# A hybrid recurrent layer on one core: a PSUM bank for the merges of the inverses, the last norm in three groups, another order of rows in the output product

## The chip, the cores and the metric

The kernel runs on one core of one Trainium2 chip. The metric is the device time of one execution in microseconds, smaller is better; comparisons use the median of several runs.

## The reference

One layer over a prompt of 1024 tokens and 8 sample tokens that go on from carried states, D = 1024:

```
h = RMSNorm(x);  p = h @ W_in
mixed = concat[GLA(p), S5(p), GatedDeltaNet(p), RWKV7(p)]     # 256 columns each, each times SiLU of its own gate path
x = x + mixed @ W_out
y = RMSNorm(x) * final_g
```

All four mixers are causal recurrences over the tokens. GatedDeltaNet (GDN) and RWKV7 are computed in chunks of 64 tokens; each chunk needs the inverse of a unit triangular 64 x 64 matrix. The outputs are y for all 1032 tokens and the last states of every mixer.

## The kernel before

**Tiling.** The tokens are taken in two halves: 512, and 512 plus the 8 samples (520). In the code the second half's steps are marked by an apostrophe. Every product with a weight matrix is a *stream* (`stream`, L269): a weight slice of 1024 x 128 is loaded in two chunks of four blocks (256 KB each), split by ScalarE (`wh`, L265) and GpSimd (`wl`, L266) into a high and a low part, and multiplied in three passes, 24 matmuls for each piece of columns (L277). With 520 columns there are two pieces of 260 and 48 matmuls. `proj` streams the normed input; `out_stream` (L1272) streams the gated branch outputs against W_out, transposes the result back and hands it on.

**Stages.** Each mixer is made of units (R RWKV, D GDN, L GLA, S S5), two pairs of heads each, that run in stages: 0 projections, 1 preparation, 2 the inverse, 3 the scan over chunks (GLA: stage 2 is the scan). A gate `g` is visited twice: first its projection, then the norm of the branch output and its product with the gate (`gated`, L1210). W is the preparation of the S5 weights, `x` the norm of the input, `T` the output product (`tail_first` for the first half, `tail` for the second), `y` the scaling of the first half's rows (`rows_first`). `x'` loads its rows with an order constraint behind the last matmul issued before it, and its result `xhi` takes the one buffer that the first half's projections read.

**Order.** The string ORDER (L33) is the order in which the stages are written down, and with that their priority; PRI (L32) raises single stages by a number of places. A planner built into the framework then lays out the queue of each engine from priorities, from dependencies and from the buffers of each tag that are free (NB, L25). So the order on an engine isn't the order of the string, and each engine works off its own queue strictly in order.

**Inverses.** `inverse` (L287) inverts the 32 x 32 diagonal blocks on VectorE (31 steps, L307 and L309), sends them through DRAM into XT, transposes them into Dn (L318), and merges them: for each of two 64-row groups p a product `pq` (L323), a copy (L324), a product `po` (L326) and a copy into XT (L327). There are 8 inverses (two pairs of RWKV and GDN in two halves). `pq` and `po` are tiles of the psc pool, which has four PSUM banks; the scans of RWKV, GDN and GLA (L471 to L501, L679 to L704, L820 to L829) and the transposes of the output streams (L1282) use the same pool. Of the eight banks two are for psp (streams), two for psb.

**The end.** In `tail` (L1320) the result of each of 8 output streams is added to x in columns of 128 (L1345). After the seventh stream (896 columns) `squares` sums squares on ScalarE and multiplies by final_g on VectorE; after the eighth it does so for the last 128 columns. Then the norm's factor is made on five small columns, each row group is scaled and stored.

The matmuls in a stream take the 128-row blocks k of the branch outputs in the order 0 to 7: GLA (0, 1), S5 (2, 3), GDN (4, 5), RWKV (6, 7). Before the matmuls `out_parts` splits each block into ohi (L1268) and olo; its loop order GORD is RWKV, GDN, GLA, S5.

Of the kernel before, what the change touches and what calls it, by code (L numbers as in the profile page):

```python
# [8 lines left out]
F32 = mybir.dt.float32  # L9
F32R = mybir.dt.float32r  # L10
I32 = mybir.dt.int32
AF = mybir.ActivationFunctionType
ALU = mybir.AluOpType
# [9 lines left out]
HALF = T // 2  # L23
NH = HALF + NS
NB = dict(ta=9, pr=11, on=3, gp=8, sh=2, kA=6, XT=2, Gt=5, s8=4, ss=4, wr=3, wh=2, wl=2, d1=1, LT=1, DT=2, DP=1, d2=2, Dn=2, w8=2, rf=1,  # L25
          fx=3, bv=2, Bn=2, UV=2, r=3, dr=2, gcn=2, ben=2, kdn=2, U=3, at=2, s5i=1, s5h=3, nst=2, psp=2, psb=2, psc=4)
CT_WA, CT_R, CT_SM, CT_G, CT_L, CT_U, CT_GATE = 0, 1, 7, 8, 14, 20, 22
GLA, S5, GDN, RWKV = 0, 1, 2, 3
ENG = dict(kqo="G", kqi="G", qd="G", kds="V", kd="G", rga="G", rgm="V", rcos="G", k2="V", ari="V", aro="V", bko="G", bki="V",
           glu="V", g5="V", cvm="V", l2="V", sgl1="V", sgl2="V", lw0="V", lw1="G", ld0="G", ld1="G", lqk="V", rS="A", rr="V",  # L30
           rU="V", dU="V", fg="V", la="V", tlo="V", cv0="V")
PRI = {"R2": 4000, "D2": 1000, "R3": 4000, "D3": 4000, "L1": 2000, "R1": 600, "L0": 100, "L2": 600, "D0": 300, "D1": 1000}  # L32
ORDER = ("x W W t W m R0 g6 R0 D0 W W M W D0 D1 R1 W R0 R1 R0 L0 R1 L0 R1 D1 L0 g0 D0 D0 S g0 L1 g4 g6 D1 g3 g7 L1 D1 g2 g5 L1 "  # L33
         "x' g7 g1 g4 S t' R1' R1' m' R0' g1 g2 R1' g3 M' R1' R0' D0' g5 R0' D1' D0' L1' g1' g7' R0' D0' D1' g4' g6' D0' L0' L1' "
         "L1' D1' g2' g7' g0' L0' S' D1' g6' g4' L0' g5' g3' S' g3' g0' g1' g5' g2' T y T'")
GORD = ((RWKV, 0), (RWKV, 1), (GDN, 0), (GDN, 1), (GLA, 0), (GLA, 1), (S5, 0), (S5, 1))
GATES = ((GLA, 0), (GLA, 1), (S5, 0), (S5, 1), (GDN, 0), (GDN, 1), (RWKV, 0), (RWKV, 1))
LEVELS = (16, 8, 4, 2, 1)
# [25 lines left out]
def trunk(ctx: ExitStack, tc: tile.TileContext, I, O):  # L64
# [195 lines left out]
    def wsplit(src):  # L260
        raw = wst.tile([128, 4, 128], F32, tag="wr", bufs=NB["wr"], name="wr")
        SP.dma_start(out=raw, in_=src)
        hi = wst.tile([128, 4, 128], F32R, tag="wh", bufs=NB["wh"], name="wh")
        lo = wst.tile([128, 4, 128], F32R, tag="wl", bufs=NB["wl"], name="wl")
        A.copy(hi, raw)  # L265
        G.tensor_tensor(lo, raw, hi, ALU.subtract)  # L266
        return hi, lo

    def stream(wsrc, evac):  # L269

        wt = [wsplit(wsrc[:, 4 * q:4 * q + 4, :]) for q in range(2)]
        for c0, m in X["pieces"] or pieces(X["n"]):
            p = ps_p.tile([128, 512], F32, tag="p", name="psp")
            for k in range(8):
                hi, lo = wt[k // 4]
                for s, (w, x) in enumerate(((hi, X["hi"]), (hi, X["lo"]), (lo, X["hi"]))):
                    X["mm"] = PE.matmul(p[:, :m], w[:, k % 4, :], x[:, k, c0:c0 + m], start=(k == 0 and s == 0), stop=(k == 7 and s == 2))  # L277
            evac(p[:, :m], c0, m)

    def proj(ct, evac):  # L280
# [6 lines left out]
    def inverse(Ga, XT, after):  # L287


        Q = [(p, f) for p in range(2) for f in range(2)]  # L290
        at = lambda p, f: slice(64 * p + 32 * f, 64 * p + 32 * f + 32)
        d1 = drp.tile([2, 2, 8, 32, 32], F32, tag="d1", bufs=NB["d1"], name="d1")
        for p, f in Q:
            r = slice(32 * f, 32 * f + 32)
            nb = 8 // len(Ga[p])
            for b, g in enumerate(Ga[p]):
                SP.dma_start(out=d1[p, f, nb * b:nb * b + nb].rearrange("(c e) s t -> s c e t", e=2), in_=g[r, :, :, r])
        LT = tmp.tile([128, 32, 32], F32, tag="LT", bufs=NB["LT"], name="LT")
# [12 lines left out]
        for q in range(4):  # L311
            SP.dma_start(out=d2.rearrange("p f x (m q) i -> q (p f x) m i", q=4)[q], in_=DT[32 * q:32 * q + 32])
        for p, f in Q:
            SP.dma_start(out=XT[at(p, f), :, 32 * f:32 * f + 32], in_=d2[p, f].rearrange("x c i -> c x i"))
        Dn = tmp.tile([128, 8, 32], F32, tag="Dn", bufs=NB["Dn"], name="Dn")
        for p in range(2):
            late(G.memset(XT[at(p, 1), :, 0:32], 0.0), after)
            V.transpose(Dn[at(p, 0)], XT[at(p, 0), :, 0:32])  # L318
        pq = psc(128, 8, 32)
        po = psc(128, 8, 32)  # L320
        for p in range(2):
            for k in range(8):
                PE.matmul(pq[at(p, 1), k, :], Ga[p][k // nb][0:32, k % nb // 2, k % 2, 32:64], Dn[at(p, 0), k, :], start=True, stop=True)  # L323
            A.copy(Dn[at(p, 1)], pq[at(p, 1)])  # L324
            for k in range(8):
                PE.matmul(po[at(p, 0), k, :], Dn[at(p, 1), k, :], XT[at(p, 1), k, 32:64], start=True, stop=True)  # L326
            A.copy(XT[at(p, 0), :, 32:64], po[at(p, 0)])  # L327
# [944 lines left out]
    def out_stream(m):  # L1272

        yT = tmp.tile([128, NH], F32, tag="sh", bufs=NB["sh"], name="yT")

        def evac(p, c0, k):
            A.copy(yT[:, c0:c0 + k], p)

        stream(I["wo"][m], evac)
        pt = psc(128, 4, 128)  # L1280
        for j in range(4):
            PE.transpose(pt[:, j, :], yT[:, 128 * j:128 * j + 128], ident)  # L1282
        return yT, pt
# [36 lines left out]
    def tail(fgb):  # L1320
        n = NH
        out_parts(1)
        xf = [big(128, D, name="xf") for _ in range(4)]
        for j in range(4):
            late(SP.dma_start(out=xf[j], in_=I["x"][HALF + 128 * j:HALF + 128 * j + 128, :]), X["mm"])
        xs = tmp.tile([128, D], F32, tag="kA", bufs=NB["kA"], name="xs")
        late(SP.dma_start(out=xs[:NS], in_=I["x"][T:TT, :]), X["mm"])
        G1 = 896
        st = tmp.tile([128, 2, 2, 16, 1], F32, tag="nst", bufs=NB["nst"], name="nst")
        rows = [(xf[j], j, 128) for j in range(4)] + [(xs[:NS], 4, NS)]  # L1330

        def squares(g):

            cols = slice(0, G1) if g == 0 else slice(G1, D)
            for x, j, k in rows:
                junk = tmp.tile([128, D], mybir.dt.bfloat16, tag="ta", bufs=NB["ta"], name="junk")
                act(junk[:k, cols], x[:, cols], AF.Square, accum_out=st[:k, 0, g, j])
                tt("fg", x[:, cols], x[:, cols], fgb[:k, cols])

        V.memset(st[:, 0, :, 4], 1.0)  # L1340
        for m in range(8):
            yT, pt = out_stream(m)
            cols = slice(128 * m, 128 * m + 128)
            for j in range(4):
                V.tensor_tensor(xf[j][:, cols], pt[:, j, :], xf[j][:, cols], ALU.add)  # L1345
            pt = psb(128, 128)
            PE.transpose(pt[0:NS], yT[:, HALF:NH], ident)
            V.tensor_tensor(xs[:NS, cols], pt[0:NS], xs[:NS, cols], ALU.add)
            if m == G1 // 128 - 1:
                squares(0)  # L1350
        squares(1)
        w = len(rows)
        ms, t, y = st[:, 0, 0, :w, 0], st[:, 0, 1, :w, 0], st[:, 1, 0, :w, 0]
        V.tensor_tensor(ms, ms, t, ALU.add)
        V.tensor_scalar(ms, ms, 1.0 / D, EPS, ALU.mult, ALU.add)
        rsqrt_small(y, ms, t)
        for x, j, k in rows:
            if j % 2:
                V.tensor_scalar(x, x, y[:k, j:j + 1], None, ALU.mult)
            else:  # L1360
                act(x, x, AF.Copy, scale=y[:k, j:j + 1])
            SP.dma_start(out=O["y"][HALF + 128 * j:HALF + 128 * j + k, :], in_=x)
# [193 lines left out]
```

## Time and profile before

| what | value |
|---|---|
| median of 3 runs | 1075.07 us (1072.87 to 1081.68) |
| the profiled execution | 1080.05 us, its span 1078.3 us |
| TensorE, busy share of the span | 87% |
| TensorE, mean granted clock | 0.847 |
| VectorE / ScalarE / GpSimd, busy share | 65% / 43% / 37% |
| share of the chain that ended last: stream matmuls on TensorE | 20% |
| moved to and from HBM | 95.91 MB, 89 GB/s on average |

The span is the time from the first to the last instruction of the profiled execution. The granted clock is the share of TensorE's full speed (2.4 GHz; the lower level is 1.2) that it was given, averaged over a stretch. A busy TensorE at half clock does half the work.

### The profile page before, as it was taken

To read this page: it belongs to the slowest core of one execution; us is meant where nothing else is said; L and a number is where in the kernel's file an instruction comes from. 1 tells how busy PE (TensorE), PEld (TensorE's weight loads), DVE (VectorE), ACT (ScalarE), POOL (GpSimd) and SP (SyncE) were. 2 spreads that over 40 slices of the span, in tenths; PEclk is the share of its full clock that TensorE was granted. 3 is DMA by queue.
4 is the path that set the end of the run, shared out by engine and by line. 5 is a ranking of instruction groups with operands and counts; after the bars stand their busy time and mean duration, and the time that the engine had idled before them with its cause. 6 is when DMAs were issued, how large, how long until landed. Compare 5 with 4: busy or idle time off the path is not lost.

```text
span 1078.3 us, 17024 instructions
## 1 busy us (share of the span) xinstructions
PE 939.4 (87%) x5994; PEld 770.5 (71%) x5994; DVE 699.1 (65%) x1841; ACT 464.2 (43%) x1079; POOL 394.9 (37%) x434
## 2 busy tenths in 40 slices
PE   3898889979999698897999899988989989797694
PEld 3676657658767486797788777677868967685694
DVE  8628884767636954737578999878975354615614
ACT  4354543322534434532663454554225244257234
POOL 2788653531211441125264313124426311422141
PEclk9999988876868866798999898788889678998697
DMA  7133414220202132134123223211122034536422
GB/s 233 50 129 104 122 53 106 69 59 15 74 25 55 49 99 79 42 116 148 57 80 101 85 76 84 83 41 54 50 69 71 22 118 130 154 112 211 164 79 89
DMA packets 85109, 95.91 MB, mean 89 GB/s; under 512 B 41640, under 2 KB 52016, under 8 KB 85024
## 3 DMA queue, kind: packets, MB, share of 16 engines
q1 hardware_dynamic: 85024, 94.83, 28.3%
q8 instruction: 47, 0.77, 0.3%
q14 instruction: 38, 0.31, 0.1%
HBM read 75.95 MB, written 16.72 MB: 86 GB/s over the span
## 4 chain that ended last, share of the span: by engine, by line
PE 40%; DVE 21%; DMA 4%; ACT 3%; issue 2%; SPq 1%; POOL 0%; ACTq 0%; DVEq 0%
PE psp L277 20%; PE psc L690 3%; DVE DP L307 3%; PE psb L763 3%; DVE DT L309 2%; PE psc L484 2%; DVE zt L1133 1%; PE psb L1150 1%; PE psc L820 1%; PE psc L326 1%; PE psb L1149 1%; PE psb L1101 1%; DMA rot<-sX 1%; PE psb L784 1%; DVE mv L224 1%
## 5 line engine op out<-in xcount | busy, mean ns | idle before, releaser
L266 POOL TENSOR_TENSOR wl<-wr,wh 128x512 fp32r<-128x512 f32 x152 | 204.3, 1346 | 434.0 <-ACT wh L265 383.5
L277 PE MATMUL psp<-xhi,wh 128*128 128x260 f32 (+2 forms) x728 | 263.9, 363 | 10.6 <-DVE rx L356 6.5
L277 PE MATMUL psp<-xhi,wl 128*128 128x260 f32 (+2 forms) x728 | 259.0, 358 | 5.9 <-POOL wl L266 5.5
L277 PE MATMUL psp<-xlo,wh 128*128 128x260 f32 (+2 forms) x728 | 255.0, 351 | 0.7 <-DVE xlo L257 0.7
L277 PEld LDWEIGHTS psp<-xhi,wh 128*128 128x128 f32 x728 | 154.4, 212 | 33.7 <-issue 12.6
L277 PEld LDWEIGHTS psp<-xhi,wl 128*128 128x128 f32 x728 | 153.3, 212 | 27.1 <-POOL wl L266 8.6
L277 PEld LDWEIGHTS psp<-xlo,wh 128*128 128x128 f32 x728 | 154.6, 212 | 16.8 <-issue 3.8
L265 ACT CAST wh<-wr 128x512 fp32r<-128x512 f32 x152 | 93.7, 618 | 158.3 <-PE psp L277 85.4
L307 DVE TENSOR_TENSOR DP<-DT,LT 128x60 f32<-128x60 f32 (+24 forms) x248 | 82.4, 332 | 14.0 <-DMA LT<-d 4.9
L309 DVE TENSOR_TENSOR DT<-DT,DP 128x60 f32<-128x60 f32 (+24 forms) x248 | 74.4, 300 | 6.1
L277 PE MATMUL psp<-ohi,wh 128*128 128x260 f32 (+1 forms) x192 | 65.9, 346 | 10.1 <-ACT ohi L1268 8.0
L277 PE MATMUL psp<-olo,wh 128*128 128x260 f32 (+1 forms) x192 | 65.4, 341 | 0.7 <-DVE olo L116 0.7
L277 PE MATMUL psp<-ohi,wl 128*128 128x260 f32 (+1 forms) x192 | 64.1, 340 | 0.8 <-POOL wl L266 0.8
L277 PEld LDWEIGHTS psp<-ohi,wh 128*128 128x128 f32 x192 | 38.1, 200 | 13.4 <-ACT ohi L1268 8.2
L763 PE MATMUL psb<-W 64*128 64x64 f32 x256 | 41.3, 338 | 1.5 <-DVE DT L309 1.5
L112 ACT ACTIVATE eg<-eg 128x260 f32<-128x260 f32 (+1 forms) x72 | 34.2, 486 | 19.2 <-DVE eg L199 18.1
L277 PEld LDWEIGHTS psp<-olo,wh 128*128 128x128 f32 x192 | 38.3, 199 | 4.3 <-DVE olo L116 1.6
L277 PEld LDWEIGHTS psp<-ohi,wl 128*128 128x128 f32 x192 | 37.9, 200 | 3.7 <-POOL wl L266 1.5
L763 PEld LDWEIGHTS psb<-W 64*128 64x128 f32 x256 | 36.9, 244 | 5.0 <-issue 2.4
L484 PE MATMUL psc<-UV,Gt 64*128 64x64 f32 (+1 forms) x256 | 37.0, 295 | 0.6 <-ACT UV L477 0.6
L484 PEld LDWEIGHTS psc<-UV,Gt 64*128 64x128 f32 (+1 forms) x256 | 28.2, 193 | 12.6 <-issue 6.0
L116 POOL TENSOR_TENSOR df<-cum 128x256 f32<-128x256 f32 x48 | 30.6, 659 | 17.0 <-DVE cum L738 15.2
(429 smaller groups left out, 1856.5 us busy)
## 6 DMA issues: line engine op xcount, KB each, us to landing
wr<-in_wct SPq DMA_DIRECT2D x120, 256.0 KB
wr<-in_wo SPq DMA_DIRECT2D x32, 256.0 KB
xn<-in_x SPq DMA_DIRECT2D x8, 512.0 KB
LT<-d SPq DMA_DIRECT2D x32, 128.0 KB
dgp<-gp SPq DMA_DIRECT2D x8, 256.0 KB
Gml<-dG SPq DMA_DIRECT2D x4, 512.0 KB
csT<-dph SPq DMA_DIRECT2D x4, 512.0 KB
dTl<-dT SPq DMA_DIRECT2D x4, 512.0 KB
```

The source lines that it names most:

```text
L112: A.activation(out, in_, func, bias=bias, scale=scale, **kw)
L116: return (G if ENG[name] == "G" else V).tensor_tensor(out, a, b, op)
L224: V.tensor_tensor(t, S, bc8(col), ALU.mult)
L265: A.copy(hi, raw)
L266: G.tensor_tensor(lo, raw, hi, ALU.subtract)
L277: X["mm"] = PE.matmul(p[:, :m], w[:, k % 4, :], x[:, k, c0:c0 + m], start=(k == 0 and s == 0), stop=(k == 7 and s == 2))
L307: V.tensor_tensor(tp[:, :m, :w], DT[:, :m, j:j + 1].to_broadcast([128, m, w]), LT[:, j:j + 1, j + 1:32].to_broadcast([128, m, w]), ALU.mult)
L309: V.tensor_tensor(DT[:, :m, j + 1:32], DT[:, :m, j + 1:32], tp[:, :m, :w], ALU.add)
L326: PE.matmul(po[at(p, 0), k, :], Dn[at(p, 1), k, :], XT[at(p, 1), k, 32:64], start=True, stop=True)
L484: PE.matmul(o, l, r, start=start, stop=True, skip_group_check=True)
L690: PE.matmul(o, l, r, start=start, stop=True, skip_group_check=True)
L763: PE.matmul(pg[:, c, :], W[HS[e], t], W[HS[e], t].rearrange("p (b f s) -> p f b s", f=2, s=s)[:, 1], start=True, stop=True)
```

## The change

Four things are changed.

- **Merges.** A new pool `ps_i` holds one PSUM bank; `pq` and `po` become the two halves of one tile in it. The psc pool goes from four banks to three.
- **Output product.** `stream` takes an order of blocks, and `out_stream` passes 6, 7, 4, 5, 0, 1, 2, 3 (RWKV, GDN, GLA, S5). The two weight chunks are loaded in the order in which they are used.
- **Last norm.** The columns are squared and multiplied by final_g in three groups (512 after the fourth stream, 384 after the seventh, 128 after the eighth). The product of the last group is made on GpSimd, and one more small sum joins the third group's squares. The scaling of the 8 sample rows moves from ScalarE to VectorE.
- **Order.** In ORDER one W moves ahead of `m`, the first half's R0 and R1 stages swap places with L0, the projection of g5 moves behind `x'`, the end of g1 moves behind `L1'`, and `D1'` (the scan) and `g6'` move ahead of `L0'` and `S'`. In PRI, D2 goes from 1000 to 2000, D3 from 4000 to 2000, L1 from 2000 to 1600.

```diff
-          fx=3, bv=2, ..., nst=2, psp=2, psb=2, psc=4)
+          fx=3, bv=2, ..., nst=2, psp=2, psb=2, psc=3)
...
-PRI = {"R2": 4000, "D2": 1000, "R3": 4000, "D3": 4000, "L1": 2000, "R1": 600, "L0": 100, "L2": 600, "D0": 300, "D1": 1000}
-ORDER = ("x W W t W m R0 g6 R0 D0 W W M W D0 D1 R1 W R0 R1 R0 L0 R1 L0 R1 D1 L0 g0 D0 D0 S g0 L1 g4 g6 D1 g3 g7 L1 D1 g2 g5 L1 "
-         "x' g7 g1 g4 S t' R1' R1' m' R0' g1 g2 R1' g3 M' R1' R0' D0' g5 R0' D1' D0' L1' g1' g7' R0' D0' D1' g4' g6' D0' L0' L1' "
-         "L1' D1' g2' g7' g0' L0' S' D1' g6' g4' L0' g5' g3' S' g3' g0' g1' g5' g2' T y T'")
+PRI = {"R2": 4000, "D2": 2000, "R3": 4000, "D3": 2000, "L1": 1600, "R1": 600, "L0": 100, "L2": 600, "D0": 300, "D1": 1000}
+ORDER = ("x W W t W W m R0 g6 R0 D0 W W M D0 D1 R1 W R0 R1 L0 R1 R0 L0 R1 D1 L0 g0 D0 D0 S g0 L1 g4 g6 D1 g3 g7 L1 D1 g2 L1 x' "
+         "g7 g1 g5 g4 S t' R1' R1' m' R0' g2 R1' g3 M' R1' R0' D0' g5 R0' D1' D0' L1' g1 g1' g7' R0' D0' D1' g4' g6' D0' L0' L1' "
+         "L1' D1' g2' g7' g0' D1' L0' g6' S' g4' L0' g5' g3' S' g3' g0' g1' g5' g2' T y T'")
...
+    ps_i = pool("ps_i", bufs=1, space=bass.MemoryType.PSUM)
...
-    def stream(wsrc, evac):
-        wt = [wsplit(wsrc[:, 4 * q:4 * q + 4, :]) for q in range(2)]
+    def stream(wsrc, evac, order=range(8)):
+        wt = {q: wsplit(wsrc[:, 4 * q:4 * q + 4, :]) for q in dict.fromkeys(k // 4 for k in order)}
...
-            for k in range(8):
+            for i, k in enumerate(order):
...
-        pq = psc(128, 8, 32)
-        po = psc(128, 8, 32)
+        pi = ps_i.tile([128, 2, 8, 32], F32, tag="i", name="psi")
+        pq, po = pi[:, 0], pi[:, 1]
...
-        stream(I["wo"][m], evac)
+        stream(I["wo"][m], evac, [2 * b + p for b, p in GORD])
...
-        G1 = 896
-        st = tmp.tile([128, 2, 2, 16, 1], F32, tag="nst", bufs=NB["nst"], name="nst")
+        groups = {3: slice(0, 512), 6: slice(512, 896), 7: slice(896, D)}
+        st = tmp.tile([128, 4, 16, 1], F32, tag="nst", bufs=NB["nst"], name="nst")
...
-            cols = slice(0, G1) if g == 0 else slice(G1, D)
+            cols = groups[g]
...
-                act(junk[:k, cols], x[:, cols], AF.Square, accum_out=st[:k, 0, g, j])
-                tt("fg", x[:, cols], x[:, cols], fgb[:k, cols])
+                act(junk[:k, cols], x[:, cols], AF.Square, accum_out=st[:k, (3, 6, 7).index(g), j])
+                (G if g == 7 else V).tensor_tensor(x[:, cols], x[:, cols], fgb[:k, cols], ALU.mult)
...
-            if m == G1 // 128 - 1:
-                squares(0)
-        squares(1)
+            if m in groups:
+                squares(m)
...
+        V.tensor_tensor(ms, ms, u, ALU.add)
...
-            if j % 2:
+            if j % 2 or j == 4:
```

## Rows read from the trace of the kernel before

**Rows 1.** Page, part 1: busy us, share of the span, instructions.

```profile
PE 939.4 (87%) x5994; PEld 770.5 (71%) x5994; DVE 699.1 (65%) x1841; ACT 464.2 (43%) x1079; POOL 394.9 (37%) x434
```

**Rows 2.** Windows: us; busy (instructions) by engine; clock, DMA share, GB/s.

```profile
418.00:452.00 34.00, 29.91 (x208) 24.78 (x207) 24.10 (x72) 15.77 (x42) 1.67 (x3) 0.65 0.23 75
829.00:893.00 64.00, 59.06 (x392) 51.65 (x389) 32.03 (x94) 23.87 (x63) 17.79 (x20) 0.73 0.29 90
985.00:1021.00 36.00, 20.07 (x97) 16.74 (x96) 26.25 (x74) 15.14 (x49) 3.70 (x3) 0.67 0.58 215
1021.00:1027.30 6.30, 6.30 (x56) 6.28 (x55) 1.07 (x5) 1.89 (x4) 2.58 (x3) 1.00 0.28 86
```

**Rows 3.** Timeline of TensorE, 1004 to 1015: start, us, what [idle before].

```profile
1004.41 0.80 PE L277 MATMUL psp<-ohi,wh 128*128 128x260 f32 x2 [0.97 <-ACT ohi L1268]
...
1009.15 0.60 PE L1237 MATMUL psb<-constA,on 128*128 128x128 f32 x4
...
1014.96 0.59 PE L277 MATMUL psp<-ohi,wh 128*128 128x260 f32 x1 [4.82 <-ACT ohi L1268]
```

**Rows 4.** Timeline of VectorE, 1005 to 1015.

```profile
1005.01 0.68 DVE L1208 TENSOR_TENSOR on<-on,nst 128x512 f32<-128x512 f32 x1
...
1007.58 5.88 DVE L1316 SCALAR_TENSOR_TENSOR yr<-yr,nst,fgb 128x1024 f32<-128x1024 f32 x4
...
1013.38 0.87 DVE L1249 SCALAR_TENSOR_TENSOR gp<-psb,constA,gp 128x512 f32<-128x512 f32 x2
```

**Rows 5.** Timeline of ScalarE, 989 to 1015: the casts of ohi.

```profile
989.67 0.61 ACT L1268 CAST ohi<-gp 128x520 fp32r<-128x520 f32 x1
...
990.29 1.13 ACT L1268 CAST ohi<-gp 128x520 fp32r<-128x520 f32 x2
...
1014.29 0.62 ACT L1268 CAST ohi<-gp 128x520 fp32r<-128x520 f32 x1 [4.51 <-DVE gp L1249]
```

**Rows 6.** Timeline of VectorE: the second transposes into Dn of three inverses.

```profile
287.54 0.44 DVE L318 STREAM_TRANSPOSE Dn<-XT 32x256 f32<-32x256 f32 x1
...
385.72 0.43 DVE L318 STREAM_TRANSPOSE Dn<-XT 32x256 f32<-32x256 f32 x1
...
774.51 0.44 DVE L318 STREAM_TRANSPOSE Dn<-XT 32x256 f32<-32x256 f32 x1
```

**Rows 7.** Timeline of TensorE: merges of those inverses, scans behind them.

```profile
337.60 0.69 PE L323 MATMUL psc<-Dn,Gg 32*32 32x32 f32 x16
...
338.73 0.69 PE L323 MATMUL psc<-Dn,Gg 32*32 32x32 f32 x16 [0.45 <-ACT Dn L324]
...
418.73 0.69 PE L323 MATMUL psc<-Dn,Gg 32*32 32x32 f32 x16
...
424.51 0.69 PE L690 MATMUL psc<-r,XT 64*64 64x64 f32 x4
...
828.66 0.69 PE L323 MATMUL psc<-Dn,Gg 32*32 32x32 f32 x16
...
842.36 0.68 PE L690 MATMUL psc<-r,XT 64*64 64x64 f32 x4
```

**Rows 8.** Timeline of ScalarE, 338: the copy after the first merge product.

```profile
338.32 0.36 ACT L324 COPY Dn<-psc 32x256 f32<-32x256 f32 x1 [1.74 <-PE psc L323]
```

**Rows 9.** Timeline of ScalarE, then of VectorE, 1059 to 1067.

```profile
1059.55 0.95 ACT L112 ACTIVATE junk<-xf 128x896 bf16<-128x896 f32 x1 [1.64 <-DVE xf L1345]
...
1064.23 0.62 ACT L1277 COPY yT<-psp 128x260 f32<-128x260 f32 x2
...
1060.62 4.10 DVE L116 TENSOR_TENSOR xf<-xf,fgb 128x896 f32<-128x896 f32 x4 [0.33 <-ACT junk L112]
...
1065.64 0.87 DVE L1345 TENSOR_TENSOR xf<-psc,xf 128x128 f32<-128x128 f32 x4
...
1066.63 0.92 DVE L116 TENSOR_TENSOR xf<-xf,fgb 128x128 f32<-128x128 f32 x4
```

**Rows 10.** Groups by line: names, shapes, count; busy us, mean ns; idle before.

```profile
L704 ACT COPY on<-psc 64x128 f32<-64x128 f32 x32 | 8.3, 260 | 44.3 <-DVE state L703 40.4 <-PE psb L1237 3.6
```

More of the change, by code (lines that the diff above doesn't have):

```diff
@@ L25 @@
 NB = dict(ta=9, pr=11, on=3, gp=8, sh=2, kA=6, XT=2, Gt=5, s8=4, ss=4, wr=3, wh=2, wl=2, d1=1, LT=1, DT=2, DP=1, d2=2, Dn=2, w8=2, rf=1,
-          fx=3, bv=2, Bn=2, UV=2, r=3, dr=2, gcn=2, ben=2, kdn=2, U=3, at=2, s5i=1, s5h=3, nst=2, psp=2, psb=2, psc=4)
+          fx=3, bv=2, Bn=2, UV=2, r=3, dr=2, gcn=2, ben=2, kdn=2, U=3, at=2, s5i=1, s5h=3, nst=2, psp=2, psb=2, psc=3)
 CT_WA, CT_R, CT_SM, CT_G, CT_L, CT_U, CT_GATE = 0, 1, 7, 8, 14, 20, 22
@@ L267, in wsplit @@
         return hi, lo
-    def stream(wsrc, evac):
-        wt = [wsplit(wsrc[:, 4 * q:4 * q + 4, :]) for q in range(2)]
+    def stream(wsrc, evac, order=range(8)):
+        wt = {q: wsplit(wsrc[:, 4 * q:4 * q + 4, :]) for q in dict.fromkeys(k // 4 for k in order)}
         for c0, m in X["pieces"] or pieces(X["n"]):
             p = ps_p.tile([128, 512], F32, tag="p", name="psp")
-            for k in range(8):
+            for i, k in enumerate(order):
                 hi, lo = wt[k // 4]
                 for s, (w, x) in enumerate(((hi, X["hi"]), (hi, X["lo"]), (lo, X["hi"]))):
-                    X["mm"] = PE.matmul(p[:, :m], w[:, k % 4, :], x[:, k, c0:c0 + m], start=(k == 0 and s == 0), stop=(k == 7 and s == 2))
+                    X["mm"] = PE.matmul(p[:, :m], w[:, k % 4, :], x[:, k, c0:c0 + m], start=(i == 0 and s == 0), stop=(i == 7 and s == 2))
             evac(p[:, :m], c0, m)
@@ L1327, in tail @@
         late(SP.dma_start(out=xs[:NS], in_=I["x"][T:TT, :]), X["mm"])
-        G1 = 896
-        st = tmp.tile([128, 2, 2, 16, 1], F32, tag="nst", bufs=NB["nst"], name="nst")
+        groups = {3: slice(0, 512), 6: slice(512, 896), 7: slice(896, D)}
+        st = tmp.tile([128, 4, 16, 1], F32, tag="nst", bufs=NB["nst"], name="nst")
         rows = [(xf[j], j, 128) for j in range(4)] + [(xs[:NS], 4, NS)]
         def squares(g):
-            cols = slice(0, G1) if g == 0 else slice(G1, D)
+            cols = groups[g]
             for x, j, k in rows:
                 junk = tmp.tile([128, D], mybir.dt.bfloat16, tag="ta", bufs=NB["ta"], name="junk")
-                act(junk[:k, cols], x[:, cols], AF.Square, accum_out=st[:k, 0, g, j])
-                tt("fg", x[:, cols], x[:, cols], fgb[:k, cols])
-        V.memset(st[:, 0, :, 4], 1.0)
+                act(junk[:k, cols], x[:, cols], AF.Square, accum_out=st[:k, (3, 6, 7).index(g), j])
+                (G if g == 7 else V).tensor_tensor(x[:, cols], x[:, cols], fgb[:k, cols], ALU.mult)
+        V.memset(st[:, 0:3, 4], 1.0)
         for m in range(8):
@@ L1348, in tail @@
             V.tensor_tensor(xs[:NS, cols], pt[0:NS], xs[:NS, cols], ALU.add)
-            if m == G1 // 128 - 1:
-                squares(0)
-        squares(1)
+            if m in groups:
+                squares(m)
         w = len(rows)
-        ms, t, y = st[:, 0, 0, :w, 0], st[:, 0, 1, :w, 0], st[:, 1, 0, :w, 0]
+        ms, t, u, y = (st[:, i, :w, 0] for i in range(4))
         V.tensor_tensor(ms, ms, t, ALU.add)
+        V.tensor_tensor(ms, ms, u, ALU.add)
         V.tensor_scalar(ms, ms, 1.0 / D, EPS, ALU.mult, ALU.add)
```

## Prediction

> **What bounds the kernel now.** I read the page first: TensorE is busy for 87% of the span [rows 1]. The next engine, VectorE, is at 65%. A kernel like that gains in two ways only: where TensorE stands still, and where it runs at the lower of its two clocks. So the second view is the table of windows [rows 2], and the reader should put three kinds of stretch beside each other. In the steady last output streams (1021 to 1027.3) TensorE is busy for all 6.30 us at a granted clock of 1.00: nothing is to be had there but less work. From 829 to 893 it is busy for 59.06 of 64 us. Two stretches are different. At the turn from the first half of the sequence to the second (418 to 452) the engine seems busy, 29.91 of 34 us, but at a clock of 0.65: worked back to full clock that is 29.91 x 0.65 = 19.4 us of work, so 14.6 us is the most that the turn can give. Between the two output stages (985 to 1021) it is busy for 20.07 of 36 us at 0.67, or 13.4 us of work: 22.6 us at most.
>
> The third view is the timeline of the second hole. TensorE waits 4.82 us until 1014.96 for a cast of ohi [rows 3]; the cast runs at 1014.29, while three others had ended by 991.4 [rows 5]. Counting matmuls between the stalls, 30 run from 1004.41 and 18 remain at 1014.96, so the missing row is the sixth of eight in the order 0 to 7: pair 1 of GDN (the fifth token from the end of ORDER, g5'). Its norm is done at 1005.69, yet its product with the gate is at 1013.38, because its transposes stand on TensorE's queue behind stream matmuls until 1009.15, and by then four rows of the first output half hold VectorE for 5.88 us from 1007.58 [rows 3, 4].
>
> The fourth view is the merges. In the inverses the transposed blocks Dn lie ready at 287.98, 386.15 and 774.95 [rows 6], but the first merge matmuls run at 337.60, 418.73 and 828.66 [rows 7]: 50, 33 and 54 us later. In each case that is when the scan ahead (RWKV pair 1, GDN pair 0, GDN pair 0 of the second half) hands out its last psc buffers. VectorE, ScalarE and TensorE all did other work in between, so what was missing was a free buffer; I infer this, no row names it. The scan behind the second and the third takes its first full product with XT at 424.51 and 842.36.
>
> The last view is the end [rows 9]: after the last stream come squares, a product with final_g, a norm and stores, all in series.
>
> **The change part by part.**
>
> *Last norm.* Before, the group of 896 columns costs ScalarE 0.95 us a row from 1059.55 and VectorE 4.10/4 = 1.03 us a row until 1064.72; the copy of the last stream waits behind the squares until 1064.23, and the sums start at 1065.64. After, that group is 384 columns. Between 0.23 us a row for 128 columns (0.92/4) and 1.03 for 896 a row costs 0.50 us, and the fifth row (8 tokens) as much: five rows end 2.6 us earlier, and the copies no longer wait. I take 0.9 us, what copy and sums can move up before TensorE's own end holds them. The product of the last 128 columns moves to GpSimd, behind nothing (its weight splits are over); VectorE loses 0.92 us after the sums, but ScalarE's squares of the same columns need nearly as long, so 0.4 us is left of it, less one more small sum of 0.2. The scale of the 8 tokens moves to VectorE beside stores that are issued one after the other: 0. Together -1.1. The 512 columns at the fourth stream cost ScalarE and VectorE 5 x 0.56 = 2.8 us each, laid into a stream in which they are busy for 1.89 and 1.07 of 6.30 us [rows 2]: 0, and if all the squares stand in front of the next weight cast, +2.8.
>
> *Order of the output streams.* RWKV, GDN, GLA, S5: the two RWKV rows and GDN pair 0 are cast first [rows 5], so 18 matmuls run in the hole. No stream matmul can then stand in front of the transposes of GDN pair 1, since all that are left wait for it. From 1005.69: transposes 0.60, products 0.87, a step of 0.04 to the cast and 0.67 from the cast to the matmul give 1007.9 in place of 1014.96, -7.1, provided the four rows of VectorE come behind; that is their place in program order. But behind that matmul now stand 30 of the 48, GLA and S5 with it, not 18. A steady stream does 56 in 6.30 us, 0.11 each; at half clock 0.225, so 12 x 0.225 = +2.7. Sum -4.4. Bounds: +2.7 if the four rows stay in front; -22.6 if the hole closes altogether. Weight chunks are loaded in the new order too, so SP's queue keeps its length.
>
> *A bank of their own for the merges.* The merges no longer wait for a psc buffer. The third lies in a stretch where TensorE is nearly full, so its 13.7 us (828.66 to 842.36) are 0 on the path. The second lies in the turn: 424.51 less 418.73, 5.8 us in which the only work left is this scan and the norm of the second half. Moving the projection of g5 behind the loads of the second half lets that norm start without waiting for its last matmul; the projection fills TensorE meanwhile, and its two weight loads of 256 KB move behind the six loads for that norm on SP's queue. For both I take half of what the turn can give, -7.3 (bounds -14.6 and +4: the loads wait for kA buffers that the same scan holds, and a projection run later holds the second half's xhi back).
>
> *What it costs.* Both products of a merge now share one bank. The row of a merge shows what that means: the second pq product starts at 338.73, as the copy of the first ends (0.36 us from 338.32), although it writes other partitions [rows 7, 8]. With po in the same bank one more such copy stands in the chain of a merge. Six merges have a scan ahead that hides it; the first of each half has none: 2 x 0.36 = +0.7 (bounds 0 and, two copies in all eight, +5.8). The Trainium skill, "PSUM — Partial Sum Buffer", section "PSUM bank collisions raise a hardware error", says that two engines may be in one bank at once if they are in different quadrants of 32 partitions; by it this term would be 0 and the sum 0.7 lower. The row shows the wait all the same, so here the program asks for more than the chip does.
>
> The scans and the output transposes keep three psc buffers, where they had four, or two while a merge ran. The nearest price is a step that waits for one copy of its predecessor, 0.26 us [rows 10]. There are 64 RWKV and GDN steps: 0 to +16.6. Since three hold this step, the next and a transpose, I take 0.
>
> *The rest of the order and the priorities.* A step of the S5 weights goes earlier in the first 60 us (VectorE and GpSimd work, two stores on SP), g1's end later, GDN's second scan ahead of S5 and GLA; D3 loses priority, D2 gains. No row prices them; TensorE is full there [rows 2]: 0, and 4 us either way.
>
> **Sum.** -1.1 - 4.4 - 7.3 + 0.7 = -12.1 us on the profiled execution of 1080.05 (span 1078.3 and 1.75 around it), so 1068.0. That execution lies 5.0 above the median of the runs, 1075.07; set against the median, 1063.0, which I forecast.
>
> **The rivals.**
> 1. *Only the end moves.* The turn is set by the kA buffers and the loads, the merges wait less but nothing on TensorE's path does: -1.1 - 4.4 + 0.7, 1070.3. For it: TensorE is at 59 of 64 us around the third merge. Against it: the clock of 0.65 in the turn.
> 2. *The last row stays last.* VectorE still does its four rows in front of GDN pair 1 and 30 matmuls follow: +2.7 - 1.1 + 0.7, with nothing from the turn 1077.4. For it: that is how the queue lies now. Against it: what pushed the transposes back is gone.
> 3. *Slower: three buffers are too few.* With two scans and a stream's transposes at once a step waits for the copy before it. It decides, above 1085.8, once it costs 15.5 us against the -4.8 of rival 1, that is 60 of 64 steps at one copy each, or 30 at two. All 64: 1070.3 + 16.6 = 1086.9. For it: the merges show that psc ran out with four. Against it: the merges themselves asked for two of these.
>
> **How the numbers follow.** Forecast 0.50, rival 1 0.28, rival 2 0.10, rival 3 0.12. Forecast's own range is 1049 (turn and hole give 12 and 13) to 1067. For 8 in 10 I leave out the tail of both ends: 1049 to 1081, with part of rival 3 outside. A time is faster by over 1% below 1064.3 and slower above 1085.8, about what can be told from no change. The forecast lies just inside faster; half of rival 1's spread and a little of rival 2's could fall there, part of the forecast's outside: 0.49 faster, 0.40 same, 0.11 slower.
>
> **What would show it.** Right: first merge matmuls within a few us of Dn in all eight inverses; from 418 to 452 a clock well over 0.65; no wait near 4.8 us in front of the first output stream, whose first 18 matmuls run before the transposes of GDN pair 1; the sums of the last stream within 1.3 us of its last matmul. Wrong: the same clock in the turn (rival 1), four rows of yr in front of the last gate (rival 2), steps of a scan that stand until a copy of on has ended (rival 3).

## The result, and the profile after

The changed kernel takes 1054.47 us (median; 1053.91 to 1059.90) against 1075.07; the ratio is 0.9866, with a 95% interval from 0.9825 to 0.9908. That is 14.4 us of 1075.07 (9.9 to 18.8), inside the forecast range and 8.5 us below the forecast of 1063.0. A ratio leaves disturbed runs of both kernels out and is taken within one session, so it is not the quotient of two medians; the median of the kernel before lay between 1074.53 and 1080.44 from session to session.

The profiled execution took 1059.90 us, span 1058.1, 20.2 less than the span of 1078.3 before. The page, part 1, as in [rows 1]:

```profile
PE 929.8 (88%) x5994; PEld 764.5 (72%) x5994; DVE 698.9 (66%) x1843; ACT 462.4 (44%) x1088; POOL 391.1 (37%) x439
```

TensorE was without work for 1078.3 - 939.4 = 138.9 us and is now for 1058.1 - 929.8 = 128.3 us; its busy time fell by 9.6 us with the same 5994 matmuls, so it was granted more clock on the whole (0.847 to 0.854). In this pair of executions the gain is half idle time, half clock. The clock half is not certain: in single runs the kernel before was granted anything from 0.832 (1095.66 us) to 0.869 (1062.19 us).

The windows (us; busy and instructions by engine; clock, DMA share, GB/s), first and second as in [rows 2]:

```profile
418.00:452.00 34.00, 26.26 (x119) 20.93 (x118) 25.77 (x78) 16.59 (x42) 2.17 (x3) 0.52 0.21 73
829.00:893.00 64.00, 59.12 (x400) 49.84 (x397) 39.21 (x105) 28.74 (x77) 21.39 (x21) 0.84 0.42 134
970.00:1000.00 30.00, 13.89 (x71) 11.75 (x70) 22.94 (x67) 9.91 (x33) 1.28 (x1) 0.66 0.49 189
```

Read the first row against [rows 2]. The turn between the halves was to come out at a clock well over 0.65; it came out at 0.52. The stretch holds 26.26 x 0.52 = 13.7 us of work, not 19.4. The turn is not where the gain is. The second row holds more: it is as busy as before (59.06 then), but at 0.84 in place of 0.73, so 49.7 us of work in place of 43.1, in the stretch that the forecast called nearly full. This row by itself does not place the gain there: of the runs below, e1, slower than the kernel before, was granted 0.90 in the same window while busy for 57.08 us, and e7, which keeps the new order, 0.77. The third row is the hole: 13.89 of 30 us at 0.66, where it was 20.07 of 36 at 0.67.

The timeline of TensorE at the third merge, and the first product of the scan behind it (start, us, what), answers [rows 7]:

```profile
777.39 0.69 PE L324 MATMUL psi<-Dn,Gg 32*32 32x32 f32 x16
...
785.43 0.69 PE L324 MATMUL psi<-Dn,Gg 32*32 32x32 f32 x16
...
788.56 0.69 PE L327 MATMUL psi<-XT,Dn 32*32 32x32 f32 x16
```

```profile
825.43 0.44 PE L691 MATMUL psc<-r,XT 64*64 64x64 f32 x4
```

Dn is ready at 775.0 in both kernels; the first merge matmul came 54 us later before, now 2.4. The scan's first full product with XT moves from 842.36 to 825.43; 8.1 of these 16.9 us are there already when the scan ahead of it ends (829.0 before, 820.9 now). All eight inverses merge within 5 us of Dn now.

The timeline of TensorE, then of VectorE, in the hole between the output stages, answers [rows 3, 4]:

```profile
974.75 0.22 PE L1243 MATMUL psb<-constA,onst 8*128 8x8 f32 x1 [0.45 <-DVE onst L1209]
980.66 1.08 PE L1238 MATMUL psb<-constA,on 128*128 128x128 f32 x4 [5.69 <-DVE nst L194]
...
988.33 0.80 PE L278 MATMUL psp<-ohi,wh 128*128 128x260 f32 x2 [1.52 <-ACT ohi L1269]
993.47 0.58 PE L278 MATMUL psp<-olo,wh 128*128 128x260 f32 x1 [4.33 <-DVE olo L117]
```

```profile
987.93 4.87 DVE L1317 SCALAR_TENSOR_TENSOR yr<-yr,nst,fgb 128x1024 f32<-128x1024 f32 x4
992.72 0.69 DVE L117 TENSOR_TENSOR olo<-gp,ohi 128x520 fp32r<-128x520 f32 x1
```

The hole is shorter, and still there. A wait of 4.33 us stands where one of 4.82 stood, for another reason: the four rows of yr (4.87 us) have slipped in front of the low part of the last block. The eight casts of ohi began at 989.7 and the last at 1014.3 before; now (one line of ScalarE: duration ns min, median, max; first and last start):

```profile
L1269 ACT CAST ohi<-gp x8: 608/624/626, 969.6 to 987.7; 128x520 fp32r<-128x520 f32 x8
```

The end, timelines of VectorE and GpSimd, answers [rows 9]:

```profile
1045.48 0.89 DVE L1346 TENSOR_TENSOR xf<-psc,xf 128x128 f32<-128x128 f32 x4 [1.46 <-PE psc L1283]
...
1047.41 0.17 DVE L1355 TENSOR_TENSOR nst<-nst 128x5 f32<-128x5 f32 x1 [0.86 <-ACT junk L113]
```

```profile
1046.29 1.69 POOL L1339 TENSOR_TENSOR xf<-xf,fgb 128x128 f32<-128x128 f32 x4 [6.11 <-ACT junk L113]
```

From the last stream matmul (1044.54) to the end of the span it is 13.6 us in place of 14.9. The column sums of the last stream start at 1045.48; GpSimd's product (1.69 us) lies beside the small sums from 1047.41.

Put side by side, the two profiled executions part like this:

| point in the trace | before | after | lead |
|---|---|---|---|
| end of the second RWKV scan, second half | 757.9 | 753.5 | 4.4 |
| end of the first GDN scan, second half | 829.0 | 820.9 | 8.1 |
| end of the second GDN scan, second half | 915.3 | 897.1 | 18.2 |
| last projection matmul | 894.0 | 883.2 | 10.8 |
| last cast of ohi | 1014.9 | 988.3 | 26.6 |
| last output matmul | 1063.4 | 1044.5 | 18.8 |
| end of the span | 1078.3 | 1058.1 | 20.2 |

So 10.8 us come before the projections end, 8.0 between there and the last output matmul, 1.3 in the last norm. The sum, 20.2, is that of two single executions and lies above the interval of the ratio (9.9 to 18.8).

### The profile page after: what moved, and what is told of

Its sections match the earlier page's. It is cut to its first block, busy times and chain, and to the rows that moved or that the text cites. A ratio compares the mean times of both kernels' runs of the same rounds, so it can differ in the third digit from the quotient of the medians.

```text
span 1058.1 us, 17042 instructions
## 1 busy us (share of the span) xinstructions
PE 929.8 (88%) x5994; PEld 764.5 (72%) x5994; DVE 698.9 (66%) x1843; ACT 462.4 (44%) x1088; POOL 391.1 (37%) x439
## 5 line engine op out<-in xcount | busy, mean ns | idle before, releaser
L267 POOL TENSOR_TENSOR wl<-wr,wh 128x512 fp32r<-128x512 f32 x152 | 207.4, 1366 | 430.8 <-ACT wh L266 376.4
L278 PE MATMUL psp<-xhi,wl 128*128 128x260 f32 (+2 forms) x728 | 254.0, 352 | 7.1 <-POOL wl L267 6.9
L278 PEld LDWEIGHTS psp<-xhi,wl 128*128 128x128 f32 x728 | 150.9, 208 | 26.3 <-POOL wl L267 10.9
L278 PEld LDWEIGHTS psp<-xlo,wh 128*128 128x128 f32 x728 | 152.6, 210 | 16.6 <-issue 4.4
L308 DVE TENSOR_TENSOR DP<-DT,LT 128x60 f32<-128x60 f32 (+24 forms) x248 | 76.2, 307 | 11.5 <-DMA LT<-d 5.5
L310 DVE TENSOR_TENSOR DT<-DT,DP 128x60 f32<-128x60 f32 (+24 forms) x248 | 77.0, 311 | 6.2
L113 ACT ACTIVATE eg<-eg 128x260 f32<-128x260 f32 (+1 forms) x72 | 33.8, 485 | 18.7 <-DVE eg L200 18.2
L485 PE MATMUL psc<-UV,Gt 64*128 64x64 f32 (+1 forms) x256 | 39.8, 292 | 2.1 <-ACT UV L478 2.1
L117 POOL TENSOR_TENSOR df<-cum 128x256 f32<-128x256 f32 x48 | 30.4, 654 | 19.7 <-DVE cum L739 12.5
L764 PE MATMUL psb<-W 64*128 64x64 f32 x256 | 34.8, 319 | 0.1
L256 PE MATMUL psb<-constA,xn 128*128 128x128 f32 (+1 forms) x72 | 15.8, 375 | 20.3 <-DVE xn L252 9.9
```

The source lines that it names most:

```text
L113: A.activation(out, in_, func, bias=bias, scale=scale, **kw)
L117: return (G if ENG[name] == "G" else V).tensor_tensor(out, a, b, op)
L256: PE.transpose(pt[:, k, :n], xn[:n, (4 * b + k) * 128:(4 * b + k + 1) * 128], ident[:n, :n])
L485: PE.matmul(o, l, r, start=start, stop=True, skip_group_check=True)
L764: PE.matmul(pg[:, c, :], W[HS[e], t], W[HS[e], t].rearrange("p (b f s) -> p f b s", f=2, s=s)[:, 1], start=True, stop=True)
```

## The experiments

Twelve variants were run. "lead of the projections" below is how much earlier than in the kernel before (894.0) the last projection matmul ends in the profiled execution; a minus means later. It is one execution each: e7 and e8 change only what stands behind the projections, and their leads of 13.2 and 7.4 beside 10.8 show how far single executions differ.

| run | what it is | ratio to before (95%) | lead of the projections, us |
|---|---|---|---|
| the change | all parts | 0.9866 (0.9825 to 0.9908) | 10.8 |
| e1 | before + own bank | 1.0134 (1.0052 to 1.0216) | -14.8 |
| e2 | before + new ORDER and PRI | 1.0301 (1.0203 to 1.0398) | -26.3 |
| f1 | before + one swap in ORDER | 1.0495 (1.0416 to 1.0574) | -34.9 |
| e5 | change, merges back in psc | 1.0226 (1.0147 to 1.0304) | -25.5 |
| e6 | change, old ORDER and PRI | 1.0023 (0.9962 to 1.0084) | -5.1 |
| f2 | e6 + the swap | 1.0174 (1.0064 to 1.0284) | -4.9 |
| f3 | change, old PRI | 0.9933 (0.9892 to 0.9974) | 6.5 |
| f5 | change, D1' moved back | 0.9966 (0.9922 to 1.0011) | 14.4 |
| e10 | change, g5 moved back | 0.9969 (0.9920 to 1.0017) | -1.2 |
| e7 | change, old order of blocks | 0.9947 (0.9898 to 0.9997) | 13.2 |
| e8 | change, yr rows later | 0.9878 (0.9788 to 0.9968) | 7.4 |
| e9 | change, two psc buffers | 1.0123 (1.0071 to 1.0176) | -8.3 |

**Each half of the change alone.** Theory A: the bank makes the gain. B: the order does. C: only the end moves. First the bank alone:

```diff
-  ..., psp=2, psb=2, psc=4)
+  ..., psp=2, psb=2, psc=3)
+    ps_i = pool("ps_i", bufs=1, space=bass.MemoryType.PSUM)
-        pq = psc(128, 8, 32)
-        po = psc(128, 8, 32)
+        pi = ps_i.tile([128, 2, 8, 32], F32, tag="i", name="psi")
+        pq, po = pi[:, 0], pi[:, 1]
```

> The kernel before, with one edit: the products of the merges stand in a PSUM bank of their own, and psc has three buffers instead of four. Theory A (the bank makes the gain: each merge runs as soon as its block Dn is ready, so the scan behind it and, through the last GDN scan, the S5 projections start earlier): 1055 to 1065, 10 to 20 us below the kernel before; the first merge matmul stands within 5 us of Dn in all eight inverses. Theory B (the new order string and its priorities make the gain; merges that run early only wait for something else): 1071 to 1079, no change, though the merges run early. Theory C (only the end moves: order of the output streams and last norm): 1073 to 1077.

Measured: 1.0134, slower (1095.78 us). All eight merges run within 4 us of Dn, and it doesn't help. Then the order alone (the two constants, as in the diff of the change):

> The kernel before, with the new ORDER string and the new priorities alone. Theory A: 1070 to 1080, no change beyond 5 us, since the three late merges (50, 33 and 54 us behind their blocks) still wait for psc buffers; the new string may shift which merge waits. Theory B: 1060 to 1067, the order alone brings 8 to 15 us. Theory C: 1073 to 1077.

Measured: 1.0301, slower still (1110.51). Then each taken out of the changed kernel; e5 puts the lines of pq and po and psc=4 back, e6 puts the two constants back:

> The changed kernel with the merges back in the psc pool and psc back at four buffers; all else stays. Theory A: 1065 to 1073, so 10 us or more of the gain is lost, and the merge of the second GDN inverse of the second half waits again for tens of us. Theory B: 1054 to 1060, nearly nothing is lost. Theory C: 1052 to 1057.

Measured: 1.0226 (1105.00).

> The changed kernel with the ORDER string and the priorities of before; bank, last norm and order of the output streams stay. Theory A: 1054 to 1060. Theory B: 1064 to 1072. Theory C: 1052 to 1057. If the two parts need each other, both this run and the one with the new order alone stand near the kernel before.

Measured: 1.0023 (1085.45).

All three theories fall as they stand. The bank costs 1.3% in the old order and, as 1.0226 - 0.9866, is worth 3.6% in the new one; the order costs 3.0% without the bank and is worth 1.0023 - 0.9866 = 1.6% with it. Of these runs only the pair gains, on top of what the end brings (e1 to e6: 1.1%, give or take 1.0). One row of the groups by line (count, busy us, mean ns, idle before, releaser) tells why, that of the first product of the four RWKV merges, of e5 and of the changed kernel:

```profile
L323 PE MATMUL psc<-Dn,Gt 32*32 32x32 f32 x128 | 6.6, 209 | 30.4 <-DVE Dn L318 30.4
```

```profile
L324 PE MATMUL psi<-Dn,Gt 32*32 32x32 f32 x128 | 6.1, 198 | 1.2 <-DVE Dn L319 1.2
```

Without the bank TensorE stands still for 30.4 us in front of merges whose block isn't ready; with it, 1.2. One wait makes up 28.51 of the 30.4: it stands in front of the merge of RWKV pair 1 in the first half, at 228.21.

**What in the order needs the bank.** In e2 the first scan began at 242.1, 2.7 us behind the last copy of a merge, where it began at 192.6 before. The new string puts the inverse of RWKV pair 1 ahead of the scan of pair 0. Theory D: that swap is it. E: something else in the string or the priorities. f1 is the kernel before with this edit alone, f2 is e6 with the same edit:

```diff
- ... R1 W R0 R1 R0 L0 R1 L0 R1 D1 L0 ...
+ ... R1 W R0 R1 L0 R1 R0 L0 R1 D1 L0 ...
```

> The kernel before, with one edit in the first half of ORDER: the inverse of RWKV pair 1 stands ahead of the scan of pair 0 (R1 L0 R1 R0 in place of R1 R0 L0 R1). Theory D (the new order needs the bank: without it the merge of pair 1, now ahead in priority, holds psc until its block is ready, and the scan of pair 0 waits; in the run with the new order alone that scan began at 242.1, 2.7 us after the last copy of that merge, where it began at 192.6 before): 1095 to 1115, the scan of pair 0 begins behind the merge of pair 1, at 235 or later, and TensorE has a hole of some 50 us in its streams around 200 to 258. Theory E (the loss of the new order without the bank comes from its second half or from the priorities): 1070 to 1085, the scan begins before 200.

Measured: 1.0495 (1121.40). TensorE's timeline, its window of that hole, and the state updates of the first half's two RWKV scans on VectorE (first and last start), all of f1:

```profile
224.41 1.06 PE L323 MATMUL psc<-Dn,Gt 32*32 32x32 f32 x16 [21.05 <-DVE Dn L318]
...
226.16 0.69 PE L471 MATMUL psc<-constA,BK 128*128 128x128 f32 x2
```

```profile
195.30:224.40 29.10, 1.94 (x18) 1.41 (x16) 22.23 (x61) 4.09 (x7) 12.64 (x18) 0.56 0.16 40
```

```profile
L500 DVE SCALAR_TENSOR_TENSOR state<-psc,fx,state x32: 266/284/292, 237.9 to 364.7; 64x64 f32<-64x64 f32 x32
```

TensorE is busy for 1.94 of 29.10 us. Its queue is worked off strictly in order; the merge is laid at its head, its block comes at 224.4, and the scan of pair 0, whose own XT has been whole since 178.4, stands behind it. Its first transposes start at 226.16, inside the merge. Theory D holds, and the size (4.95%, about 53 us) is more than the whole loss of e2.

> The changed kernel with the ORDER and priorities of before, and in them this one swap (inverse of RWKV pair 1 ahead of the scan of pair 0). Theory D: the scan of pair 0 begins before 190 all the same, since the merge has its own bank; the time falls from 1085 (the same kernel without the swap) by the larger part of the 31 us that the new order brings: 1055 to 1070. Theory E: 1080 to 1090; the gain of the order lies in its second half or in the priorities.

```profile
L501 DVE SCALAR_TENSOR_TENSOR state<-psc,fx,state x32: 268/284/292, 185.4 to 347.1; 64x64 f32<-64x64 f32 x32
```

Measured: 1.0174 (1085.97), the first update at 185.4, 52 us earlier than in f1. So with its own bank the merge no longer stands in front of the scan. But the time does not fall below e6 (1.0023): D is right about the harm and wrong about the gain. What the new order gives lies elsewhere.

This narrows what "only the pair gains" means. The move that needs the bank is this swap, and with the bank the swap brings nothing (lead of the projections -4.9 us in f2, -5.1 in e6). The rest of the new order shows no such need: without the bank it takes the ratio from 1.0495 (f1) to 1.0301 (e2), with it from 1.0174 (f2) to 0.9866. The new order without the swap, on four psc buffers and without the bank, was not run. That a kernel of this kind gains as much as the changed one is a rival that the runs leave open.

**Where the order's gain lies.** Three parts of it were undone singly in the changed kernel. f3 takes the old PRI. f5 moves the scan D1' back:

```diff
- ... g0' D1' L0' g6' S' g4' L0' ...
+ ... g0' L0' S' D1' g6' g4' L0' ...
```

e10 moves the projection of g5 back:

```diff
- ... D1 g2 L1 x' g7 g1 g5 g4 S t' ...
+ ... D1 g2 g5 L1 x' g7 g1 g4 S t' ...
```

> The changed kernel with the priorities of before (D2 1000, D3 4000, L1 2000); the new ORDER string stays. With the own bank the new order and priorities together brought 31 us (1085 to 1054), and the swap in the first half was not it. Theory G (the priorities are it: in the run with the old ones the scan of D0' takes 82 us, 763.8 to 845.4, against 67 in the changed kernel): 1070 to 1090, scan of D0' over 75 us. Theory H (the string is it): 1052 to 1060, scan of D0' about 67 us.

Measured: 0.9933 (1069.36); scan of D0' 68.5 us, not over 75.

> The changed kernel with one move in ORDER undone: the scan D1' and g6' stand behind L0' and S' again. Theory H in its nearest form (this move brings the scan of D1', the last of the scans, 28 us forward, and with it the end of the last branches): 1065 to 1090, scan of D1' from 850 or later. Theory G: 1052 to 1060, scan of D1' from about 829. If this run and the one with the old priorities both stay near 1055, the gain lies in what is left: the step of the S5 weights that goes earlier, and the projection of g5 behind the loads of the second half.

Measured: 0.9966 (1066.83). State updates of the second half's two GDN scans on VectorE, first and last start, of the kernel before, the changed kernel, f5 and e1:

```profile
L703 DVE SCALAR_TENSOR_TENSOR state<-state,egb,psc x32: 259/280/290, 764.1 to 915.0; 64x64 f32<-64x64 f32 x32
```

```profile
L704 DVE SCALAR_TENSOR_TENSOR state<-state,egb,psc x32: 258/280/289, 753.8 to 896.8; 64x64 f32<-64x64 f32 x32
```

```profile
L704 DVE SCALAR_TENSOR_TENSOR state<-state,egb,psc x32: 258/280/289, 751.6 to 916.1; 64x64 f32<-64x64 f32 x32
```

```profile
L704 DVE SCALAR_TENSOR_TENSOR state<-state,egb,psc x32: 261/280/290, 773.5 to 945.2; 64x64 f32<-64x64 f32 x32
```

In f5 the scan of D1' starts on time (827.4) but ends at 916.4 instead of 897.1, behind L0' and S' in priority; the S5 scan then ends at 921.1 instead of 914.8 and the last cast at 992.7 instead of 988.3, although its projections end 3.6 us earlier. So this move pays behind the projections: from their end to the last output matmul it is 169.6 us in f5 and 161.3 in the changed kernel.

> The changed kernel with the projection of g5 back ahead of the loads of the second half. The forecast gave the turn between the halves 7.3 us, for this move and the second merge together: 1057 to 1063. Rival (the turn gave nothing: its clock is 0.60 after and 0.65 before, and its gap between the streams of the two halves did not shrink): 1052 to 1057.

Measured: 0.9969 (1079.50). By the ratios each costs some 0.7 to 1.0%, with an interval of about 0.6% either way. How the three rank is less sure: they ran in one session, and the median of e10 lies 10 to 13 us above those of f3 and f5. G and H are both half right; neither holds the gain alone. e10 looks like the forecast's turn term, but its place isn't the turn. The windows over stream matmuls alone (busy us, count, clock), of the kernel before, the changed kernel and e10:

```profile
0.00:500.00 500.00, 245.28 (x952) 0.83 0.27 82
0.00:700.00 700.00, 357.92 (x1704) 0.85 0.28 84
0.00:880.00 880.00, 432.99 (x2136) 0.85 0.26 80
```

```profile
0.00:500.00 500.00, 241.01 (x928) 0.83 0.29 86
0.00:700.00 700.00, 356.27 (x1704) 0.85 0.29 85
0.00:880.00 880.00, 436.19 (x2172) 0.85 0.28 82
```

```profile
0.00:500.00 500.00, 243.11 (x985) 0.85 0.29 84
0.00:700.00 700.00, 349.51 (x1704) 0.86 0.29 84
0.00:880.00 880.00, 423.29 (x2136) 0.85 0.27 78
```

At 500 us, behind the turn, e10 has done 985 stream matmuls, the kernel before 952 and the changed kernel only 928. At 700 all three stand at 1704, but that count hides a difference: behind the 1704th the streams pause for 20 to 22 us in all three. The 1704th starts at 686.8 in the kernel before, at 684.9 in the changed kernel and at 691.9 in e10. So against the kernel before, the larger part of the lead of 10.8 us is made behind that point, in the stretch with both GDN scans and the third merge. Against e10 it is not: e10 is 10.7 us ahead at the 1400th stream matmul (583.9 against 594.6) and 7.0 behind at the 1704th, and ends its projections 12.0 behind. The windows of all work from 600 to 700 (columns as in [rows 2]), of the changed kernel and of e10, show the loss:

```profile
600.00:700.00 100.00, 90.54 (x673) 73.95 (x672) 84.89 (x233) 49.41 (x116) 25.62 (x21) 0.88 0.30 85
600.00:700.00 100.00, 84.91 (x622) 69.14 (x622) 87.41 (x242) 43.74 (x105) 23.01 (x19) 0.81 0.29 81
```

TensorE is busy there for 5.6 us less, at a lower clock. An edit in the first half's string is paid some 200 us behind it. Why there, the runs do not show.

**The order of the output streams and the four rows.** e7 puts the blocks back in the order 0 to 7 (`stream` as before). e8 holds the yr rows behind the first output stream:

```diff
-            V.scalar_tensor_tensor(x, x, y[:, j:j + 1], fgb, ALU.mult, ALU.mult)
+                late(V.scalar_tensor_tensor(x, x, y[:, j:j + 1], fgb, ALU.mult, ALU.mult), after)
...
+            if m == 0:
+                rows_of_first(X["mm"])
```

> The changed kernel with the blocks of the output streams back in the order 0 to 7. The forecast gave the order of the streams 4.4 us: 1056 to 1062 here. Rival (the four rows of the first half stand in front of the last block's low part anyway, with 30 matmuls behind them in the new order and 18 in the old, so that the new order gives nothing or costs up to 2.7 us): 1050 to 1055.

Measured: 0.9947 (1066.70), so the order is worth 0.9947 - 0.9866 = 0.8%, about 9 us with an interval from 2 to 16. The casts of ohi in e7:

```profile
L1269 ACT CAST ohi<-gp x8: 607/624/629, 976.4 to 1001.0; 128x520 fp32r<-128x520 f32 x8
```

Its first cast comes 95.6 us behind its last projection matmul (880.8), 86.4 in the changed kernel; the eight take 24.6 us, and 18.1. So of the 15.7 us by which the last cast comes closer to the projections, 9.2 lie ahead of the first cast, where the output streams of the first half run. Those use the new order too: the first of them starts 1.3 us behind the last projection matmul, 6.0 in e7, which is 4.7 of the 9.2. The other 4.5 are the eight streams themselves, 83.3 us against 87.8, at a granted clock of 0.96 against 0.90; that the order makes this part, the runs do not show. Behind the last cast 6.2 us are given back: 50.0 us to the last matmul in e7, 56.2 in the changed kernel.

> The changed kernel with one addition: the four scaled rows of the first half (yr, 4.9 us on VectorE) are held behind the first output stream. In the trace of the changed kernel they stand in front of the low part of the last block, and TensorE waits 4.33 us for it. Theory F (that wait is on the path): 1049 to 1053. Rival (the rows, their four loads and stores and the buffers that they hold get into the way of the end): 1054 to 1060.

TensorE, then VectorE, in e8:

```profile
991.72 0.80 PE L278 MATMUL psp<-ohi,wh 128*128 128x260 f32 x2 [1.52 <-ACT ohi L1269]
992.46 0.58 PE L278 MATMUL psp<-olo,wh 128*128 128x260 f32 x1
```

```profile
992.32 4.86 DVE L1318 SCALAR_TENSOR_TENSOR yr<-yr,nst,fgb 128x1024 f32<-128x1024 f32 x4
```

Measured: 0.9878 (1057.58), the same as the changed kernel. The 4.33 us wait is gone, and from the last cast to the last matmul it is 51.4 us in place of 56.2. But in that execution the projections end 3.4 us later, and the 4.8 us are not to be told from the scatter of the times. Whether e8 is the better kernel stays open.

**The price of a buffer.**

> The changed kernel with two psc buffers in place of three; the eighth bank stays empty. It prices a buffer. If a buffer less costs a step of a scan one copy (0.26 us) in each of 64 steps, as the third rival of the forecast had it: 1071 or more. If steps run at most two buffers deep anyway: 1053 to 1058.

Measured: 1.0123 (1092.58): a third buffer is worth 1.0123 - 0.9866 = 2.6%, some 28 us. The Trainium skill, "Perfetto Trace Analysis", section "Optimization Strategy", says that a gap which repeats on the engine that should be saturated can mean that there is too little SBUF or PSUM for the next tile. Here the large gap of f1 does not repeat; it stands once, and its row names a late block, not a buffer.

## Why the forecast came out, and which of its steps did not

The total was right in sign and within the range. The steps behind it were not all right, and that their sum fits is in part luck: the 7.3 us written for the turn were not there, and gains that were put too low or at nothing stand in for them.

- **Last norm, -1.1.** Right: the end piece is 14.9 us in every run with the old norm and 13.6 in every run with the new one. The column sums of the last stream start 0.94 us behind its last matmul (1045.48, 1044.54), within the 1.3 that the forecast named; before it was 1065.64 against 1063.37 [rows 9]. That is the whole gain: from there to the end it is 12.6 us in both, so the 0.2 for the product on GpSimd does not show. The 512 columns cost 0.62 us a row on ScalarE and 0.69 on VectorE, not 0.56 (a line between the two costs named gives 0.63), and still nothing on the path: behind 993.47 no wait of TensorE in the output streams is longer than 0.25 us.
- **Order of the output streams, -4.4.** Right in sign, too small: -0.8%, or -9.5 us from the last projection to the last output matmul (170.8 in e7, 161.3). The term of 7.1 for the last row was mis-sized. It looked at one gate, and left out that the first half's eight streams take the same order; 9.2 of the 15.7 lie where they run. It also left out that the new place of D1' is needed: with that move undone the stretch is 169.6 us long (f5, and e6 too), with the old block order 170.8. The +2.7 for twelve more matmuls holds: 51.4 us behind the last cast in e8 against 50.0 in e7 and 48.5 before, so 1.4 to 2.9. The bound that yr stays in front came true at another place, for 4.8.
- **The turn, -7.3 for the second merge and g5.** Wrong. The clock fell to 0.52 there and the streams were behind. That undoing g5 costs 1.0%, about the size of the term, is no support for it: in the turn e10 does better (a clock of 0.70, 985 stream matmuls by 500 us against 928), and its loss appears between 600 and 700 us and behind.
- **Third merge, 0, "since TensorE is nearly full there".** This is the step that failed. With the new order the scan's products with XT start 16.9 us earlier (8.1 of it from the scan ahead) and that scan ends 18.2 us earlier; from 829 to 893 TensorE does 6.6 us more work than before, at a higher clock and equally busy. "Nearly full" was true and no bound, since it was full at a clock of 0.73 in that execution. In the order of before (e1) the bank brings no gain, as the forecast said of this merge; the forecast's error was to add up parts that do not add. How much of the pair's gain is this merge, no run isolates.
- **Merges that share a bank, +0.7.** Not to be seen in any of the eight merges. In the rows of the third merge the second pq product, at 785.43, comes 2.2 us behind the copy that it would wait for (782.87 to 783.23): it stands behind streams and scan products in TensorE's queue. The Trainium skill's rule, "PSUM — Partial Sum Buffer", section "PSUM bank collisions raise a hardware error", by which this term is 0, is neither borne out nor refuted here.
- **Three buffers, 0 (to +16.6).** The price exists. From three to two it is 2.6%. Bank and three buffers in the old order are 1.3% slower than before, which is rival 3's side: the scans of D0' and D1' take 81.5 and 78.7 us in e1 against 64.9 and 63.1. The early merge does what was asked of it there too, since the pause between the two scans falls from 23.3 to 11.7 us; the longer scans eat it up. The buffer alone is not the reason: with the same three buffers in the new order the scans take 67.1 and 67.9. Why they are long in the order of before stays open; the kernel before with three psc buffers and the merges left in them, which would price the buffer alone, was not run.
- **The rest of the order, 0 and 4 either way.** The bounds failed most clearly. One swap that wasn't priced at all costs 4.95% without the bank; PRI and the place of D1' are worth 0.7% and 1.0% with it. The forecast looked at what the moved steps cost, not at what stands behind them in a queue that is worked off in order: a merge at the head of TensorE's queue stops everything until its block comes.

Of the rivals, the third described e1 and the second named the right rows of yr; the first is refuted, since most of the gain lies before the end.

## What to carry to other kernels

Where a planner lays out in-order queues, an order and the buffers that it needs are one change: test the pair, and each without the other, before pricing either. Then undo single moves: here one swap did the harm that is seen without the bank, and with the bank it brought nothing. Ask of every step that is moved forward what its first instruction waits for and what stands behind it in that engine's queue; a row with a long idle time in front of a tiny matmul (30.4 us before 6.6 us of work) is the mark. And count what has been done by a given time (stream matmuls by 500, 700 and 880 us) before giving a gain to the place where the edit is; where a count falls into a pause that all runs have, compare the time at which it was reached.

## What was not expected of the hardware

In e6 TensorE was granted 1.00, then 0.55, then 1.00 again, while it was busy for 66.31 of 67 us (windows: us, busy and instructions by engine, clock, DMA share, GB/s):

```profile
745.00:757.00 12.00, 11.47 (x163) 10.18 (x159) 11.13 (x32) 7.07 (x20) 7.80 (x11) 1.00 0.08 23
757.00:795.00 38.00, 37.84 (x182) 32.63 (x181) 23.09 (x60) 7.01 (x16) 10.26 (x13) 0.55 0.16 44
795.00:812.00 17.00, 17.00 (x150) 13.79 (x149) 10.50 (x33) 7.62 (x21) 3.58 (x3) 1.00 0.11 33
```

In the middle stretch it is busy for 37.84 of 38 us, mostly at the lower of the two levels, 1.2 GHz; the longest wait near its start is 0.53 us, and it comes back to 2.4 GHz without a pause. The work in it is 37.84 x 0.55 = 20.8 us, so by this estimate the lower clock cost 17 us there. It is no single case: f2, whose second half is written in the same order, shows 0.64 from 757 to 795, busy for 37.30 us. Why it was given so there, the runs do not tell. It means that a full TensorE is no proof of a fast one, and that part of what a reordering gives is clock that no row of the kernel before could have promised.
